# Swapping two products at the start of a seven-product up projection, and issuing one gate convolution after a bank copy

## The chip, the core and the metric

The kernel is one program on one core of a Trainium2 chip. The core has a matrix engine (TensorE, PE in the profile; its weight loads have a row of their own, PEld), a vector engine (VectorE, DVE), an activation engine (ScalarE, ACT), a general engine (GpSimd, POOL) and a queue engine (SyncE, SP). POOL and SP also issue transfers between the chip's memory and the core. Each engine works through its own list of instructions in order, and semaphores hold an instruction back until what it needs is there. The matrix engine accumulates into eight banks, each 128 by 512 float32.

The metric is the device time of one execution in microseconds (us), the median of several runs.

## The reference, cut to what matters

One layer of a streaming encoder on 512 tokens and 2048 channels, float32. The change lies in the second half, the gated feed-forward block with a causal convolution over three tokens:

```python
h  = rms_norm(x, pre_ffn_g)
up = causal_dwconv(h @ w_up, conv_w, conv_b)          # 2 x 5632 columns
y  = (gelu(up[..., :F]) * up[..., F:]) @ w_down       # F = 5632
x  = x + rms_norm(y, post_ffn_g)
```

The convolution is per column: out[t] = b + w2 z[t] + w1 z[t-1] + w0 z[t-2].

## The kernel before

**Units and blocks.** The 5632 columns are worked in 22 units of 256. A unit u has two column blocks of `w_up`: a gate block, which gets convolution and gelu (`gate`), and a linear block, which gets the convolution and is multiplied with the gate's result (`product`, which then writes the result to memory with two POOL transfers, L977, `gd<-ca`). The first three of the 44 blocks (unit 0's two and unit 1's gate) are computed by the plain routine `up`. The other 41 are numbered k = 0 to 40 and computed by seven products each. Block 0 is unit 1's linear block, block 1 is unit 2's gate block, and so on; blocks k and k + 1 overlap in the order of the work, and blocks 0 and 1 are the first pair.

**Splitting.** To reach float32 precision each operand is split into a rounded high part and a low part (`split`, L135 on ACT for the high part, L136 on DVE for the low part). Of the seven-product stage each factor of `w_up` is split into `wfh` and `wfl`, 128 by 1024 each. These live in eight buffers, four factors at a time, and four factors are prepared ahead of the product in use: the split of a factor overwrites the buffers of the factor four before it in the order, and waits until PE has read those.

**Seven products.** With h and the weight block each cut into 2 by 2 quarters, a scheme of the Strassen kind needs seven products P1 to P7 in place of eight. Each product is 8 wide matmuls with `wfh` (L159, 128x512) and 8 narrow ones with `wfl` (L165, 128x256). In `TURNED` products (P6, P7, P4) the narrow ones come first. P1, P6, P7 and P4 of one block accumulate one after the other in the same bank, named `qa`; P5 and P3 use `qg`, P2 uses `qd`. After P1, P6 and P7 the running sum in `qa` is copied out by ACT (L1159 into `za`, L1169 into `zm`, L1173 into the second half of `zm`), because a later output needs the sum up to that point. The next product on the same bank may not start until the copy has read it. So P7 waits for the copy of P6 (L1169), and P4 for the copy of P7 (L1173).

**The order of products** is the list built in `Factors.__init__`. Each product gets a key, 7k plus a place (P1 0, P2 2, P5 4, P3 6, P6 8, P7 10, P4 12), and the list is sorted by it, except for a hand-written beginning and end. Sorted, P2 of block k + 1 (key 7k + 9) falls between P6 (7k + 8) and P7 (7k + 10) of block k. The hand-written beginning of the kernel before is (block, product) (0,1), (0,2), (0,5), (1,1), (0,3), (1,2), and then the sorted rest follows: (0,6), (0,7), (1,5), (0,4), (1,3), (2,1).

PE's order is the order of the program text. The order on ACT and DVE is set by a scheduler when the program is built; `tc.issue_after(ins)` puts the instructions traced inside it behind `ins` on `ins`'s engine.

**Weights on their way.** A factor is often the sum of weight quarters. The first quarter is loaded by SP (L1089); others are added in memory order by POOL transfers that accumulate into the same tile (L1106), each issued once the split that used the previous sum is done. Of block 0, P5, P6 and P4 share the tile `wx`: the accumulating transfer for P6 follows the low-part split of P5's factor, the one for P4 follows that of P6's. P7's factor shares the tile `wy` with P3's.

**Unit 1's gate.** `gates[1] = gate(1, normed(z))` scales the plain result into `z` (L987, DVE), and `gate` runs two ACT convolution passes (L950 into `ca`), two DVE passes for each half (L951, L952) and a gelu (L964). There is one `ca` buffer, and the gate of unit 1 can only write it when the transfers that store unit 0's result (`gd<-ca`) have read it.

Of the kernel before, what the change touches and what calls it, by code (L numbers as in the profile page):

```python
# [11 lines left out]
AF = mybir.ActivationFunctionType  # L12
# [63 lines left out]
def encoder_layer(ctx: ExitStack, tc: tile.TileContext, x, xT, vecs, rel, post_mix, post_ffn,  # L76
# [7 lines left out]
    nc = tc.nc  # L84
# [48 lines left out]
    def split(hi, lo, src, scale=None):  # L133
        if scale is None:
            rounded = nc.scalar.activation(hi, src, AF.Copy)  # L135
            rest = nc.vector.tensor_sub(lo, src, f32(hi))  # L136
        else:
            rounded = nc.scalar.activation(hi, src, AF.Copy, scale=scale)
            rest = nc.vector.scalar_tensor_tensor(lo, src, scale, f32(hi), op0=ALU.mult, op1=ALU.subtract)
        split.last, split.rest = rounded.ins, rest.ins  # L140
        return rounded.ins
# [81 lines left out]
    def qk_specs(h):  # L223
        return halves(f"q{h}", w_in, head_cols("q", h), 8, P), halves(f"k{h}", w_in, head_cols("k", h), 8, P)
# [45 lines left out]
    for h in range(1, HEADS):  # L270
        q, k = qk_specs(h)
# [63 lines left out]
    for kb in range(KD):  # L335
        i, o = divmod(kb, 8)
# [22 lines left out]
    with tc.tile_pool(name="p1", bufs=2, reuse_waits="tile") as p1:  # L359
# [31 lines left out]
        def keep(what, h, ps):  # L391

            f = t512("tmp")
            nc.vector.tensor_mul(f, ps, R)
            hi, lo = t512(what + "h", F32R), t512(what + "l", F32R)
            split(hi, lo, f)
            state[what, h] = hi, lo
# [12 lines left out]
        def head(what, h):  # L410
            keep(what, h, project(f"{what}{h}"))
# [422 lines left out]
    def raw1(name, dt=F32):  # L834
        return right_tile("raw1", name, dt)
# [107 lines left out]
    def flat(v):  # L943
        return v.rearrange("p a b -> p (a b)")

    with tc.tile_pool(name="p3", bufs=2, reuse_waits="tile") as p3:
        def taps(z, b, c):

            v = [col(V_CONV, 4 * b + i) for i in range(4)]
            nc.scalar.activation(c, z, AF.Identity, scale=v[2], bias=v[3])  # L950
            nc.vector.scalar_tensor_tensor(c[:, 1:], z[:, :S - 1], v[1], c[:, 1:], op0=ALU.mult, op1=ALU.add)  # L951
            nc.vector.scalar_tensor_tensor(c[:, 2:], z[:, :S - 2], v[0], c[:, 2:], op0=ALU.mult, op1=ALU.add)  # L952

        def new_z():
            return p3.tile([P, 2, S], F32, tag="z", bufs=1, name="z")

        def gate(u, z):
            if u == NU - 1:
                a = raw1("ca")[:, :2, :]
            else:  # L960
                a = p3.tile([P, 2, S], F32, tag="ca", bufs=1, name="ca")
            for j in range(2):
                taps(z[:, j, :], 2 * u + j, a[:, j, :])
            nc.scalar.activation(flat(a), flat(a), AF.Gelu_apprx_tanh)  # L964
            return a
# [18 lines left out]
        def normed(ps):  # L984
            z = new_z()
            for j in range(2):
                nc.vector.tensor_mul(z[:, j, :], ps[j], R)  # L987
            return z

        def up(u, p, between=()):  # L990
            ps = [bank(f"up{u}_{p}_{j}") for j in range(2)]
            between = list(between)
            for i in range(4):
                w = weights.get(f"w{p}{u}_{i}")
                factors.prefetch(4 - len(weights.specs) + weights.used)
                for kb in range(4 * i, 4 * i + 4):
                    for j in range(2):
                        mm3(ps[j], part(w, j, slice(kb % 4 * P, (kb % 4 + 1) * P)), g_both(hT, kb),
                            kb == 0, kb == KD - 1)
                step = between.pop(0) if between else None  # L1000
                if step:
                    step()
            return ps
# [19 lines left out]
        def quarter(k, t, i):  # L1023

            return tuple(hT[2 * k + i][:, :, at, :] for at in AT[t])
# [7 lines left out]
        def raw_x(name):  # L1033
            return p3.tile([P, 1024], F32, tag="x", bufs=4, name=name)
# [26 lines left out]
        def h_difference():  # L1061

            for i, v in enumerate(differences):
                split(*quarter(0, 1, i), v)

        class Factors:
# [3 lines left out]
            def __init__(self):  # L1070
                n = 2 * NU - PLAIN

                self.alone = 0, n - 1
                place_of = {1: 0, 6: 8, 2: 2, 7: 10, 5: 4, 4: 12, 3: 6}
                begin = [(0, 1), (0, 2), (0, 5), (1, 1), (0, 3), (1, 2)]
                end = [(n - 1, 5), (n - 2, 6), (n - 1, 3), (n - 1, 1), (n - 2, 7), (n - 1, 6), (n - 2, 4),
                       (n - 1, 7), (n - 1, 2), (n - 1, 4)]
                order = sorted((7 * k + at, k, i) for k in range(n) for i, at in place_of.items())  # L1080
                self.order = begin + [(k, i) for _, k, i in order if (k, i) not in begin + end] + end
                self.raw, self.made, self.loaded, self.used = {}, [], 0, 0
# [59 lines left out]
        banks, gates = {}, {}  # L1142
# [6 lines left out]
        def pair_tile(tag, n, bufs=1):  # L1149
            return p3.tile([P, n, 2, T], F32, tag=tag, bufs=bufs, name=tag)  # L1150

        def wide(v):
            return v.rearrange("p a b c -> p (a b c)")

        def keep(k, i):

            if i == 1:
                zs[k, "1"] = pair_tile("za", 1, 2)
                nc.scalar.activation(wide(zs[k, "1"]), banks[k, "a"], AF.Copy)  # L1159
            elif i == 2:  # L1160
                v = wide(zs[k, "1"])
                nc.vector.tensor_add(v, banks.pop((k, "d")), v)
            elif i == 5:
                zs[k, "5"] = raw_x("zb")[:, :S] if k == end else wide(pair_tile("zb", 1))
                nc.scalar.activation(zs[k, "5"], banks[k, "g"], AF.Copy)  # L1165
            elif i == 6:
                zs[k, "m"] = pair_tile("zm", 2)
                v = wide(zs[k, "m"][:, :1])
                nc.scalar.activation(v, banks[k, "a"], AF.Copy)  # L1169
                nc.vector.tensor_add(v, banks.pop((k, "g")), v)  # L1170
            elif i == 7:
                v = wide(zs[k, "m"][:, 1:])
                nc.scalar.activation(v, banks[k, "a"], AF.Copy)  # L1173
                nc.vector.tensor_add(v, zs.pop((k, "5")), v)
            elif i == 4:
                keep_all(k)

        def keep_all(k):
            one, m, a = zs.pop((k, "1")), zs.pop((k, "m")), banks.pop((k, "a"))
            z = new_z()  # L1180
            nc.vector.tensor_add(z[:, 0, :T], one[:, 0, 0], one[:, 0, 1])
            nc.vector.tensor_add(z[:, 1].rearrange("p (a b) -> p a b", a=2), m[:, :, 0], m[:, :, 1])
            nc.scalar.activation(z[:, 0, T:], a[:, T:], AF.Copy)
            nc.vector.tensor_add(z[:, 0, T:], a[:, :T], z[:, 0, T:])
            nc.vector.tensor_mul(flat(z), flat(z), flat(RR))
            u, p = divmod(PLAIN + k, 2)
            if p:
                product(u, gates.pop(u), z)
            else:
                gates[u] = gate(u, z)  # L1190

        def seven(k, i):
            w = factors.get()
            if i in FIRST:
                banks[k, BANK[i]] = bank(f"q{BANK[i]}_{k}")
            ps = banks[k, BANK[i]]
            mm2(ps, w, [h_factor(i, kb) for kb in range(8)], i in FIRST, i in TURNED)
# [9 lines left out]
        for i in range(2):  # L1207
            h_sums(i)
        z = up(1, 0, [spread2, lambda: product(0, gate(0, normed(ups[0])), normed(ups[1]))])
        gates[1] = gate(1, normed(z))  # L1210
        rights, firsts = [right(0, cc) for cc in range(2)], []
        for r in rights:
            next(r)
# [2 lines left out]
        def next_first():  # L1216

            cc, i = ORDER0[len(firsts)]
            r = rights[cc].send(i)
            firsts.append((firsts[0][0] if firsts else first_left(), r))  # L1220

        for k, i in factors.order:
            seven(k, i)
            keep(k, i)
            if (k, i) == factors.order[0]:
                with ExitStack() as behind:
                    for ins in factors.third:
                        behind.enter_context(tc.issue_after(ins))
                    h_difference()
            if (k, i) == (end, 6):  # L1230
                summed.close()
                pr = ctx.enter_context(tc.tile_pool(name="pr", bufs=2, side="right", reuse_waits="tile"))
            if (k, i) == (end, 6):
                next_first()
            elif (k, i) == (end - 1, 4):
                next_first()
# [4 lines left out]
    with tc.tile_pool(name="p4", bufs=2, reuse_waits="tile") as p4:  # L1241
# [180 lines left out]
        for n in ("11", "12", "21", "22"):  # L1422
            for t in range(2):
# [3 lines left out]
                if n in not_stored:  # L1427
                    v = at[:, l * C + S:(l + 1) * C]
# [56 lines left out]
```

## Time and profile before

| | us |
|---|---|
| median of 3 runs | 1875.63 |
| lowest and highest run | 1873.43, 1879.35 |
| the profiled execution | 1878.7 |
| its span, first to last instruction | 1876.9 |
| PE busy in the span | 1860.8 |
| mean granted PE clock (1 is full) | 0.997 |

In rows of the timeline the first number is the start in us from the beginning of the span, the second the duration of the group, and what stands in square brackets is the idle time before it on that engine and what released it. `PEclk` is the share of full speed that PE's clock was granted. The seven-product stage begins at 636 us of the span and ends at 1443 us.

### The profile page before, as it was taken

The page shows a single profiled execution, that of the slowest core. Times are in us where ns is not written, and L with a number is a line of the kernel's source. Part 1 is how long each engine was busy: PE and PEld are TensorE (multiplying, and loading weights), DVE is VectorE, ACT ScalarE, POOL GpSimd, SP SyncE. Part 2 cuts the span into 40 slices and gives each one's busy share as a digit, 9 for nine tenths or more (in the row PEclk, how much of TensorE's full clock was granted, in tenths as well). Part 3 has the DMA queues.
Part 4 walks back from the last instruction along what each step waited for, and adds up shares of the span by engine and source line. Part 5 has one row for each costly group of instructions (what it writes and reads, how often), then busy time and mean ns, then how long its engine had stood idle before and what let it go on. Part 6 is the DMA issues. An engine that isn't in the chain of part 4 may idle for free.

```text
span 1876.9 us, 24890 instructions
## 1 busy us (share of the span) xinstructions
PE 1860.8 (99%) x9486; PEld 1592.3 (85%) x9486; DVE 1439.5 (77%) x1631; ACT 1018.8 (54%) x1287; POOL 297.9 (16%) x400
## 2 busy tenths in 40 slices
PE   9999999999999999999999999999999999999998
PEld 7888888888889888888888888888888888888886
DVE  6555445577598888888888888888887899899876
ACT  7333333246465555666656666565655665565553
POOL 5201011100000112121221212222121011111101
PEclk9999999999999999999999999999999999999999
DMA  8799599997794779889898898988989977877785
GB/s 306 238 248 239 161 261 247 246 251 259 227 303 169 182 178 202 202 206 206 201 199 200 207 208 199 198 200 208 211 171 290 349 224 177 204 202 179 174 236 151
DMA packets 181751, 409.20 MB, mean 218 GB/s; under 512 B 11456, under 2 KB 62528, under 8 KB 176320
## 3 DMA queue, kind: packets, MB, share of 16 engines
q0 software_dynamic: 52112, 156.78, 43.8%
q1 hardware_dynamic: 129520, 250.84, 39.8%
q8 instruction: 74, 1.21, 0.3%
q14 instruction: 45, 0.37, 0.1%
HBM read 361.44 MB, written 96.47 MB: 244 GB/s over the span
## 4 chain that ended last, share of the span: by engine, by line
PE 64%; issue 2%; DMA 1%; ACT 0%; DVE 0%; POOL 0%; POOLq 0%; DVEq 0%; ACTq 0%
PE qa L159 16%; PE qa L165 8%; PE qg L159 8%; PE qg L165 4%; PE pa L154 4%; PE pa L153 4%; PE pa L151 4%; PE qd L159 4%; PE pg L154 2%; PE pg L153 2%; PE pg L151 2%; PE qd L165 2%; PE pd L154 1%; PE pd L153 1%; PE pd L151 1%
## 5 line engine op out<-in xcount | busy, mean ns | idle before, releaser
L159 PE MATMUL qa<-gT,wfh 128*128 128x512 f32 x984 | 248.0, 394 | 0.0
L135 ACT ACTIVATE wfh<-wx 128x1024 fp32r<-128x1024 f32 x164 | 173.7, 1059 | 131.2 <-PE qg L159 49.7
L136 DVE TENSOR_TENSOR wfl<-wx,wfh 128x1024 fp32r<-128x1024 f32 x164 | 200.6, 1223 | 53.7 <-ACT wfh L135 36.3
L159 PEld LDWEIGHTS qa<-gT,wfh 128*128 128x128 f32 x984 | 178.1, 190 | 32.0
L1106 POOL DMA_DIRECT2D wx<-in_w_up x122 | 104.5, 857 | 511.0 <-DVE wfl L136 473.9
L159 PE MATMUL qg<-h,wfh 128*128 128x512 f32 x656 | 162.3, 389 | 0.0
L159 PEld LDWEIGHTS qg<-h,wfh 128*128 128x128 f32 x656 | 123.1, 188 | 25.7 <-ACT zb L1165 0.2
L165 PE MATMUL qa<-gT,wfl 128*128 128x256 f32 x984 | 138.9, 284 | 4.7 <-ACT zm L1169 4.7
L136 DVE TENSOR_TENSOR bl<-b,bh 128x2048 fp32r<-128x2048 f32 x56 | 127.2, 2287 | 18.7 <-ACT bh L135 11.7
L135 ACT ACTIVATE bh<-b 128x2048 fp32r<-128x2048 f32 x56 | 106.1, 1913 | 60.2 <-DVE b L870 24.3
L165 PEld LDWEIGHTS qa<-gT,wfl 128*128 128x128 f32 x984 | 130.1, 192 | 8.9 <-ACT zm L1169 5.5
L135 ACT ACTIVATE wfh<-wy 128x1024 fp32r<-128x1024 f32 x82 | 86.9, 1060 | 92.8 <-PE qg L159 50.0
L151 PE MATMUL pa<-bh,ah 128*128 128x512 f32 x320 | 124.5, 389 | 0.0
L153 PE MATMUL pa<-bl,ah 128*128 128x512 f32 x320 | 124.5, 389 | 0.0
L154 PE MATMUL pa<-bh,al 128*128 128x512 f32 x320 | 124.5, 389 | 0.0
L136 DVE TENSOR_TENSOR wfl<-wy,wfh 128x1024 fp32r<-128x1024 f32 x82 | 100.1, 1221 | 9.7 <-ACT wfh L135 5.6
L165 PEld LDWEIGHTS qg<-h,wfl 128*128 128x128 f32 x656 | 89.5, 190 | 6.4
L136 DVE TENSOR_TENSOR wfl<-wz,wfh 128x1024 fp32r<-128x1024 f32 x41 | 50.3, 1226 | 55.7 <-PE qa L159 55.7
L165 PE MATMUL qg<-h,wfl 128*128 128x256 f32 x656 | 91.5, 282 | 0.0
L159 PE MATMUL qa<-h,wfh 128*128 128x512 f32 x328 | 82.1, 392 | 0.0
L159 PE MATMUL qd<-gT,wfh 128*128 128x512 f32 x328 | 81.1, 389 | 0.0
L938 POOL DMA_DIRECT2D sum<-part x30 | 36.2, 1207 | 262.9 <-DVE part L924 191.7
(543 smaller groups left out, 4552.8 us busy)
## 6 DMA issues: line engine op xcount, KB each, us to landing
wx<-in_w_up POOLq DMA_DIRECT2D x122, 512.0 KB, 6.3
b<-in_w_down SPq DMA_DIRECT2D x32, 1024.0 KB, 7.1
wx<-in_w_up SPq DMA_DIRECT2D x43, 512.0 KB, 5.5
wz<-in_w_up SPq DMA_DIRECT2D x41, 512.0 KB, 6.1
wy<-in_w_up SPq DMA_DIRECT2D x41, 512.0 KB, 4.6
wy<-in_w_up POOLq DMA_DIRECT2D x41, 512.0 KB, 7.0
sum<-part POOLq DMA_DIRECT2D x38, 512.0 KB, 7.8
wt<-in_w_o POOLq DMA_DIRECT2D x16, 1024.0 KB, 12.8
```

What stands on the lines that cost most here:

```text
L135: rounded = nc.scalar.activation(hi, src, AF.Copy)
L136: rest = nc.vector.tensor_sub(lo, src, f32(hi))
L151: nc.tensor.matmul(ps, l[0], r[0], start=first, stop=False, skip_group_check=onto)
L153: nc.tensor.matmul(low, l[0], r[1], start=False, stop=False, skip_group_check=onto)
L154: nc.tensor.matmul(ps, l[1], r[0], start=False, stop=last, skip_group_check=onto)
L159: nc.tensor.matmul(ps, w[0][:, kb], pairs[kb][0], start=fresh and not kb, stop=last, skip_group_check=not fresh)
L165: nc.tensor.matmul(ps[:, sl], w[1][:, kb], pair[:, sl], start=False, stop=last, skip_group_check=not fresh)
L938: nc.gpsimd.dma_start(dest, v, accum_op=ALU.add)
L1106: nc.gpsimd.dma_start(self.raw[k, what], self.block(k, m, kh), accum_op=ALU.add)
```

## The change

Two edits. The hand-written beginning loses (1,2), so that the sorted rest sets its place: the order becomes (0,1), (0,2), (0,5), (1,1), (0,3), (0,6), (1,2), (0,7), (1,5), (0,4), with P2 of block 1 between P6 and P7 of block 0. And the gate of unit 1 is no longer traced ahead of the seven-product loop: its scaled input is made there as before, but the gate itself is traced after P6 of block 0 and ordered on ACT behind the copy of P6's bank (L1169). Nothing is computed in another way, and no instruction is added or removed.

```diff
-                begin = [(0, 1), (0, 2), (0, 5), (1, 1), (0, 3), (1, 2)]
+                begin = [(0, 1), (0, 2), (0, 5), (1, 1), (0, 3)]
...
                 v = wide(zs[k, "m"][:, :1])
-                nc.scalar.activation(v, banks[k, "a"], AF.Copy)
+                keep.six = nc.scalar.activation(v, banks[k, "a"], AF.Copy).ins
                 nc.vector.tensor_add(v, banks.pop((k, "g")), v)
...
         z = up(1, 0, [spread2, lambda: product(0, gate(0, normed(ups[0])), normed(ups[1]))])
-        gates[1] = gate(1, normed(z))
+        z = normed(z)
...
         for k, i in factors.order:
             seven(k, i)
             keep(k, i)
...
+            if (k, i) == (0, 6):
+                with tc.issue_after(keep.six):
+                    gates[1] = gate(1, z)
```

On PE, from P3 of block 0 to the start of its P7. In the kernel before, `qg_5453` is block 0's P3, `qd_5522` block 1's P2, and `qa_5401` block 0's bank, first P6 (with `h_5184`), then P7 (with `gT_4460`):

```order
L159 MATMUL qg_5453<-h_5183,wfh 128x512 x8
L165 MATMUL qg_5453<-h_5183,wfl 128x256 x8
L159 MATMUL qd_5522<-gT_4462,wfh 128x512 x4
L159 MATMUL qd_5522<-gT_4463,wfh 128x512 x4
L165 MATMUL qd_5522<-gT_4462,wfl 128x256 x4
L165 MATMUL qd_5522<-gT_4463,wfl 128x256 x4
L165 MATMUL qa_5401<-h_5184,wfl 128x256 x8
L159 MATMUL qa_5401<-h_5184,wfh 128x512 x8
L165 MATMUL qa_5401<-gT_4460,wfl 128x256 x4
```

The same place in the changed kernel, where the bank of block 0 is `qa_5393`, P3's is `qg_5445` and block 1's P2 has `qd_5546`:

```order
L159 MATMUL qg_5445<-h_5183,wfh 128x512 x8
L165 MATMUL qg_5445<-h_5183,wfl 128x256 x8
L165 MATMUL qa_5393<-h_5184,wfl 128x256 x8
L159 MATMUL qa_5393<-h_5184,wfh 128x512 x8
L159 MATMUL qd_5546<-gT_4462,wfh 128x512 x4
L159 MATMUL qd_5546<-gT_4463,wfh 128x512 x4
L165 MATMUL qd_5546<-gT_4462,wfl 128x256 x4
L165 MATMUL qd_5546<-gT_4463,wfl 128x256 x4
L165 MATMUL qa_5393<-gT_4460,wfl 128x256 x4
```

P6 has moved up by one product, and P2 of block 1 now stands between P6 and P7.

On ACT, from the split of P7's factor (the first `wy`) to the copy of P7, in the kernel before; the `wx` rows are the splits of block 1's P5, block 0's P4 and block 2's P1, in this order, and the second `wy` is that of block 1's P3:

```order
L135 ACTIVATE wfh<-wy 128x1024
L1159 ACTIVATE za<-qa_5478 128x512
L135 ACTIVATE wfh<-wx 128x1024
L950 ACTIVATE ca<-z,vec 128x512 x2
L135 ACTIVATE wfh<-wx 128x1024
L135 ACTIVATE wfh<-wy 128x1024
L1169 ACTIVATE zm<-qa_5401 128x512
L964 ACTIVATE ca<-ca 128x1024
L135 ACTIVATE wfh<-wx 128x1024
L1173 ACTIVATE zm<-qa_5401 128x512
```

And in the changed kernel:

```order
L135 ACTIVATE wfh<-wy 128x1024
L1159 ACTIVATE za<-qa_5470 128x512
L135 ACTIVATE wfh<-wx 128x1024 x2
L1169 ACTIVATE zm<-qa_5393 128x512
L950 ACTIVATE ca<-z,vec 128x512 x2
L135 ACTIVATE wfh<-wy 128x1024
L135 ACTIVATE wfh<-wx 128x1024
L964 ACTIVATE ca<-ca 128x1024
L1173 ACTIVATE zm<-qa_5393 128x512
```

The convolution passes of unit 1's gate (`ca<-z,vec`) and the split of block 1's P3 factor have moved from ahead of the copy of P6 (L1169) to behind it; the split of P4's factor (the second `wx`) still stands ahead of it; the gelu (L964) has moved behind the split of block 2's P1 factor, next to the copy of P7 (L1173).

On DVE, the low-part splits and the last part of unit 0's product, in the kernel before; `wz` is the factor of block 1's P2, `wx` that of block 0's P6:

```order
L974 TENSOR_TENSOR ca<-ca,cb 128x512
L136 TENSOR_TENSOR wfl<-wz,wfh 128x1024
L951 SCALAR_TENSOR_TENSOR cb<-z,vec,cb 128x511
L1162 TENSOR_TENSOR za<-qd_5430,za 128x512
L952 SCALAR_TENSOR_TENSOR cb<-z,vec,cb 128x510
L136 TENSOR_TENSOR wfl<-wx,wfh 128x1024
L974 TENSOR_TENSOR ca<-ca,cb 128x512
```

And in the changed kernel:

```order
L974 TENSOR_TENSOR ca<-ca,cb 128x512
L136 TENSOR_TENSOR wfl<-wx,wfh 128x1024
L951 SCALAR_TENSOR_TENSOR cb<-z,vec,cb 128x511
L1162 TENSOR_TENSOR za<-qd_5423,za 128x512
L952 SCALAR_TENSOR_TENSOR cb<-z,vec,cb 128x510
L136 TENSOR_TENSOR wfl<-wz,wfh 128x1024
L974 TENSOR_TENSOR ca<-ca,cb 128x512
```

The two splits have changed places. The order of the transfers on SP and on POOL is the same in both kernels.

## The prediction

> **What bounds the kernel now.** I read the page first, then the waits of PE, then PE's and ACT's timelines around the one long wait, and last the clock and the transfers there. The page's span and PE's busy time:
>
> ```profile
> span 1876.9 us, 24890 instructions
> PE 1860.8 (99%) x9486; PEld 1592.3 (85%) x9486; DVE 1439.5 (77%) x1631; ACT 1018.8 (54%) x1287; POOL 297.9 (16%) x400
> ```
>
> PE is idle for only 16.1 us of the span, so a change pays only where it moves PE's idle time or PE's rate. The waits of PE name one such place in the seven-product stage:
>
> ```profile
> PE qa L165 <- ACT zm L1169: 4.7, 2, 3.7
> ```
>
> Two waits for the copy of P6 (L1169), 3.7 us and 1.0 us. PE's timeline shows where the long one is (P2 of block 1, then P6 narrow, P6 wide, P7 narrow, P7 wide, P5 of block 1 wide and narrow, P4 narrow):
>
> ```profile
> 649.91 2.00 PE L159 MATMUL qd<-gT,wfh 128*128 128x512 f32 x8
> ...
> 652.70 1.12 PE L165 MATMUL qa<-h,wfl 128*128 128x256 f32 x8
> 653.66 2.00 PE L159 MATMUL qa<-h,wfh 128*128 128x512 f32 x8
> 659.35 2.07 PE L165 MATMUL qa<-gT,wfl 128*128 128x256 f32 x8 [3.69 <-ACT zm L1169]
> 661.22 3.62 PE L159 MATMUL qa<-gT,wfh 128*128 128x512 f32 x8
> 664.64 2.13 PE L159 MATMUL qg<-h,wfh 128*128 128x512 f32 x8
> 666.61 1.11 PE L165 MATMUL qg<-h,wfl 128*128 128x256 f32 x8
> 667.56 1.12 PE L165 MATMUL qa<-gT,wfl 128*128 128x256 f32 x8
> ```
>
> It is P7 of block 0. Besides the idle time, the matmuls after it are long: eight narrow ones take 661.22 - 659.35 = 1.87 us where P6's took 0.96, eight wide ones 3.42 us. The second pair, which already has P2 between P6 and P7, gives the measure:
>
> ```profile
> 676.87 2.00 PE L159 MATMUL qa<-h,wfh 128*128 128x512 f32 x8
> 678.71 1.98 PE L159 MATMUL qd<-gT,wfh 128*128 128x512 f32 x8
> ...
> 681.48 1.12 PE L165 MATMUL qa<-gT,wfl 128*128 128x256 f32 x8
> ```
>
> Eight wide ones take 1.84 us, a product 2.8, and P7 starts without a wait. The clock explains the rest; the windows' last three columns are granted clock, DMA share and GB/s:
>
> ```profile
> 640.00:655.00 15.00, 15.00 (x90) 13.33 (x89) 10.41 (x13) 5.92 (x7) 4.87 (x6) 1.00 1.00 263
> ...
> 658.50:664.50 6.00, 5.15 (x16) 4.47 (x17) 4.29 (x6) 2.80 (x4) 0.87 (x1) 0.50 0.47 115
> ```
>
> After the wait PE ran at half its clock. So the wait has two prices. Idle: P6's wide matmuls are through at 653.66 + 1.84 = 655.50, P7 starts at 659.35: 3.85 us. Half rate: 1.87 - 0.96 = 0.91, 3.42 - 1.84 = 1.58 and, for P5, 1.97 - 1.84 = 0.13: 2.6 us. Together 6.5 us, 0.35% of the span.
>
> Why the copy is late is in ACT's timeline:
>
> ```profile
> 640.77 1.07 ACT L135 ACTIVATE wfh<-wz 128x1024 fp32r<-128x1024 f32 x1 [1.24 <-PE qd L159]
> ...
> 643.57 1.06 ACT L135 ACTIVATE wfh<-wx 128x1024 fp32r<-128x1024 f32 x1 [0.69 <-PE qg L159]
> ...
> 649.80 1.06 ACT L135 ACTIVATE wfh<-wy 128x1024 fp32r<-128x1024 f32 x1 [4.68 <-DMA wy<-in_w_up]
> ...
> 651.24 1.05 ACT L135 ACTIVATE wfh<-wx 128x1024 fp32r<-128x1024 f32 x1
> 655.41 1.52 ACT L950 ACTIVATE ca<-z,vec 128x512 f32<-128x512 f32 x2 [3.12 <-DMA gd<-ca]
> 656.83 1.04 ACT L135 ACTIVATE wfh<-wx 128x1024 fp32r<-128x1024 f32 x1
> 657.78 1.04 ACT L135 ACTIVATE wfh<-wy 128x1024 fp32r<-128x1024 f32 x1
> 658.73 0.57 ACT L1169 ACTIVATE zm<-qa 128x512 f32<-128x512 f32 x1
> 660.82 1.06 ACT L964 ACTIVATE ca<-ca 128x1024 f32<-128x1024 f32 x1 [1.52 <-DVE ca L952]
> 661.78 1.04 ACT L135 ACTIVATE wfh<-wx 128x1024 fp32r<-128x1024 f32 x1
> 664.88 0.60 ACT L1173 ACTIVATE zm<-qa 128x512 f32<-128x512 f32 x1 [2.06 <-PE qa L159]
> ```
>
> The bank was full at 655.5, but ACT stood until 655.41 before the gate's convolution, which waits for the store of unit 0's result, and then worked through convolution and two splits.
>
> **The change part by part.** *PE's order.* P6 takes P2's start, 649.91; P2 of block 1 follows at 652.70, P7 is due at 655.50, block 1's P5 at 658.3, P4 at 661.1 (it started at 667.56, 6.5 us later).
>
> *P6's factor, split one place earlier.* Its last quarter is an accumulating transfer on POOL:
>
> ```profile
> 634.61 0.88 POOL L1106 DMA_DIRECT2D wx<-in_w_up  x1 [23.31 <-DVE wfl L136]
> ...
> 641.66 0.86 POOL L1106 DMA_DIRECT2D wy<-in_w_up  x1 [0.93 <-DVE wfl L136]
> 646.45 0.86 POOL L1106 DMA_DIRECT2D wx<-in_w_up  x1 [3.93 <-DVE wfl L136]
> 647.06 1.74 POOL L977 DMA_DIRECT2D gd<-ca  x2
> ```
>
> The landing of the first, asked for alone, of the two stores, and of all 163 accumulating ones:
>
> ```profile
> DMA to landing us min/median/max: 6.7/6.7/6.7
> ```
>
> ```profile
> DMA to landing us min/median/max: 7.5/7.5/7.6
> ```
>
> ```profile
> DMA to landing us min/median/max: 5.3/6.6/9.6
> ```
>
> It is there at 634.61 + 6.7 = 641.3; the split ends at 642.4, its low part on DVE at about 643.7, and P6 needs both at 649.91. Cost nothing, with 6 us of cover. The transfer behind it, for P4's factor, is then issued at about 643.9 instead of 646.45. The POOL queue keeps its order (behind `wy` of 641.66, ahead of the stores), so nothing is pushed behind more bytes. SP's next load into the tile that P2's factor frees goes out about one product, 2.8 us, later; its reader stands eleven products behind, 30 us, and its queue keeps its order. Cost nothing.
>
> *The copy of P6.* Ahead of it on ACT now stand only splits: P7's (649.80, held by the transfer of 641.66, which the change leaves alone), block 1's P5 (651.24) and P4's. P4's split needs its transfer, which by the range of landings is there between 643.9 + 5.3 = 649.2 and 653.5, and P6's buffers, which PE gives up at 652.70. I take 652.9, at latest 653.6; one split (656.83 to 657.78) is 0.95, so the copy runs from 653.85 to 654.4, at latest to 655.15. P7 is due at 655.50: the wait goes, cover 0.35 to 1.1 us. With it goes its half-rate stretch, since no idle time is left ahead of it.
>
> *The gate, behind the copy.* It waits for the stores, in before until 655.41. Unit 0's last multiplication on DVE now stands behind the low part of P6's factor instead of P2's; the high part before it ends at 642.4 instead of 641.84 (640.77 + 1.07), so the stores go out up to 0.6 us later, unless the earlier transfer ahead of them helps. The gate's convolution starts between 654.4 (right behind the copy) and 656.0; I take the old 655.4. Then come 1.4 us for it, 0.95 for block 1's P3 split, and from 658.3 + 0.2 the split of block 2's P1 factor, which waits for P7's wide matmuls: until 659.45. Gelu 0.95, copy of P7 0.6: about 661.0 against P4's start at 661.1. Gelu's DVE input is no later, since two foreign instructions leave that chain:
>
> ```profile
> 646.07 0.69 DVE L974 TENSOR_TENSOR ca<-ca,cb 128x512 f32<-128x512 f32 x1
> ...
> 656.92 0.68 DVE L1162 TENSOR_TENSOR za<-qd,za 128x512 f32<-128x512 f32 x1
> ...
> 658.84 1.22 DVE L136 TENSOR_TENSOR wfl<-wx,wfh 128x1024 fp32r<-128x1024 f32 x1
> 659.98 0.74 DVE L952 SCALAR_TENSOR_TENSOR ca<-z,vec,ca 128x510 f32<-128x510 f32 x1
> ```
>
> Without them the last pass ends near 659.0 instead of 660.7. P4 may still wait between 0 and 1.9 us (gelu at its old 660.82 puts the end of P7's copy at 662.4, 1.3 late, and 0.6 for late stores). I take 0.1, nearest to the chain as added up. Who needs the gate itself is the product with block 0's result, which only follows P4's end at 663.9.
>
> *Sum.* -3.85 - 2.6 + 0.1 = -6.35 us, between -6.45 and -4.55. From 664 us on the order is the old one, and the stage ran there on PE alone but for the 1.0 us wait, so all of it arrives at the end: span 1870.5, and 1.8 us around it, 1872.3 against the profiled 1878.7. That execution lies 3.1 us above the median of the three runs and within their limits; off the median, 1875.63 - 6.35 gives 1869.3 us.
>
> [...] The rows show one wait of 3.7 us followed by 0.50 of the clock, and no second case. [...]
>
> **The rivals.** *The half-rate stretch is not in the runs that set the median.* Then only the idle 3.85 us are to be had there, less the 0.1: 1871.9. For it: a wait this short was followed by half rate in one profiled execution, and the three runs spread over 5.9 us. Against it: that execution is itself an ordinary one. [...]
>
> *The wait moves to P4.* The gate now stands between the copies of P6 and P7. If the stores land 2 us late, the chain above gives P4 a wait of some 2.5 us: 1875.63 - 6.45 + 2.5 = 1871.7. For it: transfers run at a DMA share of 1.00 from 640 to 655, and my chain has 0.1 us to spare. Against it: their bytes and order are the same.
>
> *Slower.* The split of P4's factor, which waits for a transfer, stands ahead of the copy of P6, so a late transfer holds P7. To lose 5.6 us on before, P7 must start at 655.50 + 3.85 + 5.6 = 665 (half rate as before), so the transfer must land at 663.4, 19.5 us after its issue. The longest of 163 took 9.6. It would give 1881.2 or more.
>
> **How the numbers follow.** Forecast 0.58 (1869.3, own range 1866.5 to 1872), no half rate to save 0.20, wait at P4 0.15, slower 0.07, which holds the spread of runs too. 0.3% is 5.6 us, about what a measurement of this kernel can tell from no change; the forecast clears it by 0.7 us, with runs 3 us to either side. Of the forecast's 0.58 I give 0.45 to faster and 0.13 to within; of the two partial cases together 0.10 to faster. Faster 0.55, same 0.38, slower 0.07. The range, 1865.8 to 1876.0, reaches from the whole 6.5 us with the runs 3.3 lower to no gain.
>
> **What would show it.** In the profile after: no wait of P7 at 655.5 us and no line "qa L165 <- ACT zm L1169" of 3.7 us; a clock of 1.00 from 655 to 665; P4 at 661 to 662; the copy of P6 done by 655.2; the gate's convolution at 654.4 to 656. A wait of P4 for L1173 over 1 us would show the second rival, a copy of P6 after 656 the third, and a before whose runs keep full clock after the wait the first. The forecast is wrong if the stage's end, 1443 us, comes less than 4 us earlier.

## The result

The changed kernel took 1872.2 us (median of 22 runs, 1869.37 to 1875.16); the kernel before, run beside it, 1877.13 us (22 runs, 1873.24 to 1879.37). The ratio is 0.9977, with a 95% interval of 0.9970 to 0.9983: a gain of 0.23%, or 4.3 us (3.2 to 5.6); the two medians are 4.9 us apart, the two means 4.4. So it is faster, as the interval does not reach 1, and the upper end of the gain touches the 5.6 us (0.3%) that the prediction took as about what a measurement can tell from no change. The time lies in the range given and 2.9 us above the forecast.

The page of the profiled execution of the changed kernel, and the waits of PE that are left in it:

```profile
span 1867.6 us, 24890 instructions
PE 1857.1 (99%) x9486; PEld 1590.2 (85%) x9486; DVE 1437.1 (77%) x1631; ACT 1020.2 (55%) x1287; POOL 297.8 (16%) x400
```

```profile
PE idle L128 <- DVE early L120: 1.1, 1, 1.1
PE q L151 <- ACT q_0h L135: 0.3, 1, 0.3
PE q L153 <- DVE hT L139: 0.3, 1, 0.3
```

The line of L165 waiting for L1169, 4.7 us in the kernel before, in two waits, is gone. This execution took 1869.37 us, the shortest of the 22, so the 9.3 us between it and the profiled execution of before are not the gain. PE's timeline at the place (P6 narrow and wide, P2 of block 1, P7, P5 of block 1, P4 of block 0):

```profile
648.74 1.12 PE L165 MATMUL qa<-h,wfl 128*128 128x256 f32 x8
649.70 2.00 PE L159 MATMUL qa<-h,wfh 128*128 128x512 f32 x8
651.54 1.98 PE L159 MATMUL qd<-gT,wfh 128*128 128x512 f32 x8
653.35 1.12 PE L165 MATMUL qd<-gT,wfl 128*128 128x256 f32 x8
654.30 1.12 PE L165 MATMUL qa<-gT,wfl 128*128 128x256 f32 x8
655.26 2.00 PE L159 MATMUL qa<-gT,wfh 128*128 128x512 f32 x8
657.10 1.98 PE L159 MATMUL qg<-h,wfh 128*128 128x512 f32 x8
658.92 1.11 PE L165 MATMUL qg<-h,wfl 128*128 128x256 f32 x8
659.87 1.12 PE L165 MATMUL qa<-gT,wfl 128*128 128x256 f32 x8
```

No row has a wait, the wide matmuls of P7 take 1.84 us again, and P4 starts 659.87 - 634.80 = 25.07 us after the stage's first product (P1 of block 0, at 634.80 here, 635.97 in before); in before it was 667.56 - 635.97 = 31.59 us. ACT's timeline over the same stretch:

```profile
648.96 1.05 ACT L135 ACTIVATE wfh<-wx 128x1024 fp32r<-128x1024 f32 x1
652.39 1.06 ACT L135 ACTIVATE wfh<-wx 128x1024 fp32r<-128x1024 f32 x1 [2.39 <-DMA wx<-in_w_up]
653.35 0.58 ACT L1169 ACTIVATE zm<-qa 128x512 f32<-128x512 f32 x1
653.83 1.51 ACT L950 ACTIVATE ca<-z,vec 128x512 f32<-128x512 f32 x2
655.25 1.05 ACT L135 ACTIVATE wfh<-wy 128x1024 fp32r<-128x1024 f32 x1
656.20 1.04 ACT L135 ACTIVATE wfh<-wx 128x1024 fp32r<-128x1024 f32 x1
658.04 1.06 ACT L964 ACTIVATE ca<-ca 128x1024 f32<-128x1024 f32 x1 [0.81 <-DVE ca L952]
659.01 0.58 ACT L1173 ACTIVATE zm<-qa 128x512 f32<-128x512 f32 x1
```

The copy of P6 is through at 653.93, 0.37 us ahead of P7; the gate's convolution follows right behind it; the copy of P7 is through at 659.59, 0.28 us ahead of P4. The granted clock (third number from the right) stays whole through the stretch:

```profile
655.00:658.00 3.00, 3.00 (x16) 2.52 (x15) 3.00 (x6) 2.24 (x3) 0.00 (x0) 1.00 0.92 253
658.00:661.00 3.00, 3.00 (x22) 2.83 (x21) 3.00 (x4) 2.49 (x3) 0.87 (x1) 1.00 0.16 37
```

So the mechanism came out as forecast, 6.5 us at the place between these two executions, and yet the runs differ by 4.3 us. The experiments ask where the other 2 us are.

### The profile page after: what moved, and what is told of

Read it like the earlier page. It is cut to its first block, busy times and chain, and to the rows that moved or that the text cites. A ratio compares the mean times of both kernels' runs of the same rounds, so it can differ in the third digit from the quotient of the medians.

```text
span 1867.6 us, 24890 instructions
## 1 busy us (share of the span) xinstructions
PE 1857.1 (99%) x9486; PEld 1590.2 (85%) x9486; DVE 1437.1 (77%) x1631; ACT 1020.2 (55%) x1287; POOL 297.8 (16%) x400
## 4 chain that ended last, share of the span: by engine, by line
PE 98%; DVE 1%; ACT 1%; DMA 0%; SPq 0%; issue 0%; POOL 0%; DVEq 0%; POOLq 0%; ACTq 0%
PE qa L159 16%; PE qa L165 8%; PE qg L159 8%; PE qg L165 4%; PE qd L159 4%; PE pa L153 4%; PE pa L154 4%; PE pa L151 4%; PE m L154 3%; PE m L151 3%; PE m L153 3%; PE qd L165 2%; PE pg L153 2%; PE pg L154 2%; PE pg L151 2%; PE u L151 2%
## 5 line engine op out<-in xcount | busy, mean ns | idle before, releaser
L165 PE MATMUL qa<-gT,wfl 128*128 128x256 f32 x984 | 137.7, 283 | 0.0
L165 PEld LDWEIGHTS qa<-gT,wfl 128*128 128x128 f32 x984 | 129.4, 191 | 3.4
L151 PE MATMUL pa<-bh,ah 128*128 128x512 f32 x320 | 124.5, 389 | 0.0
L165 PEld LDWEIGHTS qg<-h,wfl 128*128 128x128 f32 x656 | 89.5, 190 | 6.4
L165 PE MATMUL qg<-h,wfl 128*128 128x256 f32 x656 | 91.5, 282 | 0.0
```

The costliest lines, as they stand in the source:

```text
L151: nc.tensor.matmul(ps, l[0], r[0], start=first, stop=False, skip_group_check=onto)
L165: nc.tensor.matmul(ps[:, sl], w[1][:, kb], pair[:, sl], start=False, stop=last, skip_group_check=not fresh)
```

## The experiments

Theory A: the place costs the kernel before a different amount in each run, because its wait and the half-rate stretch vary; the change takes all of it. Theory B: the place always cost 6.5 us, and the change gives some of it back elsewhere. Theory C, for the changed kernel alone: P4 takes over some of the wait.

In what follows a profile is one profiled execution (a "look" in the expectations); "first profile" means the one of before or of the changed kernel that stands above. To compare them, each is cut at three rows of PE's timeline: the start of the stage, the start of P4 of block 0 (the place), and the first matmul of the down projection (L151, the stage's end). In the first profile of the changed kernel P7 starts 19.50 us after the stage's start and P4 25.07 us after it. "Idle" is by how much P7 starts later than those 19.50 us, "half rate" what the place costs beyond 25.07 us and the idle part. Where the clock stayed whole behind a wait, 0.08 to 0.09 us stand in this column too, since the first narrow matmuls after a wait take some 1.05 us instead of 0.96.

| execution | stage starts at | place | idle | half rate | rest of stage | from stage's end to end of span |
|---|---|---|---|---|---|---|
| before | 635.97 | 31.59 | 3.88 | 2.64 | 775.94 | 433.40 |
| same_a | 636.44 | 30.22 | 3.48 | 1.67 | 775.07 | 433.37 |
| same_b | 636.63 | 30.35 | 3.78 | 1.50 | 775.28 | 433.44 |
| same_c | 636.44 | 31.35 | 3.40 | 2.88 | 776.08 | 433.43 |
| same_d | 635.28 | 30.16 | 3.41 | 1.68 | 774.47 | 433.39 |
| same_e | 635.64 | 31.05 | 4.32 | 1.66 | 775.35 | 433.46 |
| same_f | 636.57 | 30.35 | 3.87 | 1.41 | 774.48 | 433.40 |
| fill | 637.01 | 28.64 | 3.49 | 0.08 | 774.39 | 433.36 |
| order_only | 636.50 | 27.34 | 2.18 | 0.09 | 774.41 | 433.45 |
| gate_only | 635.75 | 26.04 | 0.88 | 0.09 | 776.89 | 433.42 |
| changed | 634.80 | 25.07 | 0 | 0 | 774.30 | 433.43 |
| after_b | 638.29 | 25.08 | 0.01 | 0 | 775.71 | 433.42 |
| after_c | 636.58 | 25.07 | 0.01 | 0 | 775.90 | 433.45 |
| after_d | 635.62 | 25.07 | 0 | 0 | 775.70 | 433.41 |

**The kernel before, again (same_a).** No edit.

> The kernel before, unchanged, for a second look at its wait of P7. Theory A (the half-rate stretch depends on the moment at which the wait falls): the wait of P7 for the copy of P6 is again 3 to 4 us, but the granted clock after it may be 0.50 for some 6 us or 1.00; where it is 1.00 the place costs 3.9 us, not 6.5. Theory B (the gain of the change was real in full, 6.5 us, and about 2 us were given back behind the stage): clock 0.50 again, 6.5 us lost at the place in this look too. Time the same as before, ratio 1.000.

1876.88 us, ratio 1.0003 (0.9994 to 1.0012). The place cost 30.22 us, 1.4 us less than in the first profile of before. Half of theory A's idea shows in PE's timeline:

```profile
654.13 2.00 PE L159 MATMUL qa<-h,wfh 128*128 128x512 f32 x8
659.42 1.21 PE L165 MATMUL qa<-gT,wfl 128*128 128x256 f32 x8 [3.29 <-ACT zm L1169]
660.47 3.56 PE L159 MATMUL qa<-gT,wfh 128*128 128x512 f32 x8
663.83 2.05 PE L159 MATMUL qg<-h,wfh 128*128 128x512 f32 x8
```

The wait is nearly the same, but the eight narrow matmuls right after it still take 1.05 us; only then does the clock fall, and the wide ones take 3.36. So the half rate did not come and go, as theory A had it; it came at another moment, and cost 1.7 us in place of 2.6.

**The idle time filled (fill).** The wait stays, but PE works through most of it on zeros, into a bank of its own; the 14 matmuls are 28 records in the trace.

```diff
         for k, i in factors.order:
+            if (k, i) == (0, 7):
+                spare = bank("spare")
+                for _ in range(14):
+                    nc.tensor.matmul(spare[:, :P], early, early, start=True, stop=True)
             seven(k, i)
```

> The kernel before with 14 matmuls of 128x128 on zeros into a spare bank between P6 and P7 of block 0, so that PE works through most of its 3.85 us wait: the wait stays, the idle time goes. Theory A: no half-rate stretch; P7 starts at the same time as before; gain against a look with half rate 2.6 us, against the mean of before's runs less than that, 0.5 to 1.5 us (ratio 0.9992 to 0.9997). Theory B: gain 2.6 us (ratio 0.9986).

```profile
654.71 2.01 PE L159 MATMUL qa<-h,wfh 128*128 128x512 f32 x8
656.56 3.29 PE L1226 MATMUL spare<-early 128*128 128x128 f32 x28
660.00 1.21 PE L165 MATMUL qa<-gT,wfl 128*128 128x256 f32 x8 [0.15 <-ACT zm L1169]
661.04 2.00 PE L159 MATMUL qa<-gT,wfh 128*128 128x512 f32 x8
```

```profile
658.00:661.00 3.00, 2.85 (x25) 2.65 (x24) 3.00 (x5) 1.95 (x3) 0.00 (x0) 1.00 0.78 134
```

P7 starts as late as before (3.49 us late), and everything after it runs at full rate; the granted clock is 1.00 where the kernel before had 0.51. The ratio is 0.9996 (0.9987 to 1.0005), 11 runs against 33. That lies in theory A's range, and theory B's 0.9986 lies just outside the interval; but the interval holds no change as well as the 1.9 us that the half rate cost in the mean of the seven profiles of before. That the stretch of half rate comes from the idle time is shown by this trace, one against seven; its price is not settled by this run's time.

**The order alone (order_only).**

```diff
-                begin = [(0, 1), (0, 2), (0, 5), (1, 1), (0, 3), (1, 2)]
+                begin = [(0, 1), (0, 2), (0, 5), (1, 1), (0, 3)]
```

> Only the list is changed (P2 of block 1 between P6 and P7); the gate stays ahead of the copy of P6 on ACT. Both theories: P6 ends 2.8 us earlier and the stores land earlier, but the copy still stands behind the gate's convolution and one split; P7 waits 0.5 to 1.5 us at a clock of 1.00, so the place costs that instead of 6.5 us. Theory A: ratio 0.998 to 0.9985; theory B: 0.997 to 0.998.

```profile
655.18 1.52 ACT L950 ACTIVATE ca<-z,vec 128x512 f32<-128x512 f32 x2 [3.07 <-DMA gd<-ca]
656.61 1.04 ACT L135 ACTIVATE wfh<-wx 128x1024 fp32r<-128x1024 f32 x1
657.55 0.57 ACT L1169 ACTIVATE zm<-qa 128x512 f32<-128x512 f32 x1
```

P7 waited 2.0 us, more than the 0.5 to 1.5 expected, since the stores of unit 0's result, and the gate behind them, were hardly earlier here: the gate began 18.7 us after the stage's start, 19.4 in the first profile of before. There is no half rate in this profile, and its place is 3.4 us cheaper than the mean of before. The ratio is 0.9993 (0.9984 to 1.0002), a smaller gain than either theory had, 1.3 us (none to 3.0). In 4 of the 11 timed runs the mean granted clock was 0.997 and in those the mean time 1875.9 us, against 1874.2 us in the others. This may be half rate after a wait of some 2 us in some runs, but no trace shows it, and the mean clock is a loose sign: one run of after_b below has 0.953 at an ordinary 1873.44 us.

**The gate alone (gate_only).** `begin` as before, the rest of the change as it is.

> Only the gate is moved behind the copy of P6; P7 follows P6 directly as before. The copy can only begin when P6 ends, and the split of block 1's P3 factor, which waits for P6's buffers, stands ahead of it: P7 waits 1.0 to 2.0 us, at a clock of 1.00. Theory A: ratio 0.998 to 0.9990; theory B: 0.997 to 0.998.

```profile
654.47 1.04 ACT L135 ACTIVATE wfh<-wy 128x1024 fp32r<-128x1024 f32 x1
655.49 0.60 ACT L1169 ACTIVATE zm<-qa 128x512 f32<-128x512 f32 x1
655.98 1.51 ACT L950 ACTIVATE ca<-z,vec 128x512 f32<-128x512 f32 x2
```

The copy follows P6's end by 0.2 us, and P7 waits 0.69 us, less than expected: the split of block 1's P3 factor runs from 654.47, while P6's wide matmuls are still at work, so it does not wait for those. P6's narrow ones were through by then, at 653.45. The ratio, 0.9979 (0.9970 to 0.9988), cannot be told from that of the whole change, and it lies at the border of the two theories' ranges. The move of the gate carries most of the gain, 4.7 of the 5.65 us at the place; with the gate moved, the order adds the other 0.97 us, which no time here resolves.

**The changed kernel, again (after_b, after_c, after_d).** No edit.

> The changed kernel, unchanged, looked at again. The place (from P1 to P4 of block 0) takes 25.1 us where no wait is left, 31.6 and 30.2 us in the two looks at before; the rest of the stage took 774.3 to 775.9 us, the tail 433.4 us in every look, and the stage began at 634.8 to 637.0 us. Theory A (before's cost at the place varies with its wait and clock, the change always takes all of it): 25.1 us at the place, 774.3 for the rest; a time above that of the first look (1869.4 us) comes from a stage that begins later than 634.8 us. Theory B (part of the gain is given back): the place is 25.1 us in each look, but the rest of the stage is 775.5 to 777 us in some, by a wait of PE for ACT behind the place. Theory C: P4 waits for the copy of P7 in some looks and the place is 25.5 to 27 us.

> As for after_b: A: place 25.1, rest 774.3; B: place 25.1, rest 775.5 to 777; C: place 25.5 to 27 us.

> As for after_b: A: place 25.1, rest 774.3; B: place 25.1, rest 775.5 to 777; C: place 25.5 to 27 us.

The place is 25.07 or 25.08 us in each, and P4 never waits: theory C falls. The rest of the stage is 775.7 to 775.9 us, 1.4 to 1.6 us above the first profile, with short waits of PE behind the place, here those of after_d and after_b from 664 to 1450 us:

```profile
PE qg L159 <- ACT zb L1165: 0.9, 1, 0.9
```

```profile
PE qa L165 <- ACT zm L1169: 0.8, 2, 0.5
```

That is what theory B expected, but the kernel before has such waits too, none to 1.0 us in a profile, and the profiles of before below have the same rest. after_b was also timed: 1872.18 us, ratio 0.9977 (0.9967 to 0.9987), the same as the first time.

**Five more profiles of before (same_b to same_f).**

> The kernel before once more. If its cost at the place varies between looks (theory A): anything from 28.5 us (a wait of some 3.4 us at full clock) to 31.6 us. If it is always the whole of idle time and half rate (theory B): 30 to 31.6 us, with a clock of 0.50 for 3 to 6 us.

> The kernel before again, for what the place costs it from run to run. Three looks gave 31.6, 30.2 and 30.4 us from P1 to P4, so 5.1 to 6.5 us over the 25.1 us of the changed kernel, while the timed runs of the two kernels differ by 4.3 us (3.2 to 5.6). Theory A (the place is dearer in some runs than in others, the rest does not care): looks with 28 to 30 us must turn up, and the rest of the stage stays at 774 to 776 us. Theory B (the change gives back 1 to 2 us elsewhere): the place costs 30 to 31.6 us again, and the rest of before is 1 us shorter than that of the changed kernel (775.4 us in the mean of four looks).

> As for same_c: A: 28 to 31.6 us at the place, rest 774 to 776; B: 30 to 31.6 us, rest near 774.4.

> As for same_c: A: 28 to 31.6 us at the place, rest 774 to 776; B: 30 to 31.6 us, rest near 774.4.

> As for same_c: A: 28 to 31.6 us at the place, rest 774 to 776; B: 30 to 31.6 us, rest near 774.4.

The place cost 30.16 to 31.35 us, never less than 30. Two of them, same_c with the half rate at the wait's own end, and same_f with its end within P7's wide matmuls:

```profile
659.34 2.08 PE L165 MATMUL qa<-gT,wfl 128*128 128x256 f32 x8 [3.20 <-ACT zm L1169]
661.22 3.62 PE L159 MATMUL qa<-gT,wfh 128*128 128x512 f32 x8
664.63 2.38 PE L159 MATMUL qg<-h,wfh 128*128 128x512 f32 x8
```

```profile
659.94 2.08 PE L165 MATMUL qa<-gT,wfl 128*128 128x256 f32 x8 [3.67 <-ACT zm L1169]
661.82 2.48 PE L159 MATMUL qa<-gT,wfh 128*128 128x512 f32 x8
664.13 2.00 PE L159 MATMUL qg<-h,wfh 128*128 128x512 f32 x8
```

The granted clock of same_c and then of same_f (third number from the right) shows where the factor of two comes from:

```profile
658.00:661.00 3.00, 1.66 (x7) 1.66 (x8) 3.00 (x5) 1.48 (x3) 0.00 (x0) 0.60 0.41 81
661.00:664.00 3.00, 3.00 (x9) 2.42 (x9) 1.78 (x3) 1.80 (x2) 0.87 (x1) 0.50 0.75 195
664.00:667.00 3.00, 3.00 (x12) 2.37 (x12) 2.04 (x3) 0.60 (x1) 0.56 (x1) 0.76 0.87 160
```

```profile
658.00:661.00 3.00, 1.06 (x5) 1.06 (x6) 3.00 (x5) 1.89 (x3) 0.00 (x0) 0.73 0.52 100
661.00:664.00 3.00, 3.00 (x13) 2.58 (x13) 2.37 (x4) 2.01 (x2) 0.87 (x1) 0.70 0.52 183
664.00:667.00 3.00, 3.00 (x19) 2.62 (x18) 2.52 (x3) 1.44 (x2) 0.85 (x1) 1.00 0.96 146
```

Taking the clock as either 1.00 or 0.50 at each moment (in before it is 0.50 over the whole of 658.5 to 664.5 us), the time at half rate is 6 us times what a window lacks to 1.00, summed: (0.40 + 0.50 + 0.24) x 6 = 6.84 us in same_c, (0.27 + 0.30) x 6 = 3.42 us in same_f. The same sum gives 6.84 us for before and 3.42 us for each of the other four: in these seven profiles a stretch came in one length or in twice that length. What it cost is close to half of the part of it in which PE had work. In same_f it began at 661 - 0.27 x 6 = 659.38, 0.56 us ahead of P7, so 2.86 us were left and cost 1.43 (1.41 in the table); in same_c it began at 658.60, 0.74 us ahead of P7, and 6.10 us were left, half of which is 3.05 (2.88 in the table).

Over the seven profiles the idle part is 3.73 us in the mean and the half-rate part 1.92 (1.41 to 2.88): the place costs 30.72 us, 5.65 over the changed kernel. The profiles are from more than one chip, but same_b and after_b to after_d share one, and there the place is 30.35 against 25.07 to 25.08 us. The rest of the stage is 775.24 us in the mean of before and 775.40 of the changed kernel, the start 636.14 and 636.32 us: no give-back that could be told from their scatter, which is 1.6 us from the lowest rest to the highest in either kernel. Place, rest and start together make the profiles differ by 5.3 us, which lies in the interval of the timed runs, 3.2 to 5.6. Theory B falls in its main point, that the place always costs 6.5 us; a give-back of up to some 1 us is not ruled out. Theory A holds for the size of the half-rate part, not for its absence. Between 5.3 and the 4.3 us of the timed runs stays 1 us that these profiles do not settle.

## Why the prediction was right or wrong, point by point

- **The bound, the place and the cause.** Right. The copy of P6 stood behind the gate's convolution on ACT, the gate behind the stores; with the gate behind the copy and a product between, the wait goes, in four profiles of four. P4 was due 661.1 - 635.97 = 25.1 us after the stage's start, and came at 25.07.
- **The half-rate term.** The step that failed is the term of the sum "Half rate: ... 2.6 us", which was taken from one execution. It was one of the two largest of seven, the two in which the stretch had its double length; the mean of the seven is 1.92 us. The idle term, 3.85 us, was 3.73 in the mean. So the sum of 6.35 us was 0.7 us too large at the place.
- **From the sum to the time.** The forecast took 6.35 us off a median of three runs, 1875.63 us; 22 runs gave 1877.13. These 1.5 us are half of the 2.9 us by which the forecast lies too low; the other 1.4 are the 6.35 us of the sum against the 4.9 between the medians. With the gain at 4.3 us, 0.23%, the result is on the near side of 0.3%, which had a chance of 0.38; "faster by over 0.3%", with 0.55, did not come.
- **The cover of the copy of P6.** Right in its outcome, wrong in one of its reasons. P4's split on ACT did not wait for all of P6: in after_d it began at 651.26, while P6's wide matmuls ran from 650.52 to 652.36. Nor does such a split wait, as the section on the kernel before has it, until PE has read both buffers of the factor four before it. Here and in gate_only the split on ACT began after P6's narrow matmuls and ahead of the end of its wide ones, which fits one of the two buffers being free by then; no run tests it. P4's split was held by its transfer, which landed 9.7, 9.7, 9.8 and 7.3 us after its issue in the four profiles, in three of them past the 9.6 that I had taken as the upper end. The cover at P7 was 0.37, 0.25, 0.58 and 1.96 us, against the 0.35 to 1.1 I had worked out.
- **The gate behind the copy.** Right. It started right behind the copy in three profiles and waited 1.23 us for the stores in one; these landed 6.0 to 7.3 us after their issue instead of 7.5 to 7.6. P4's 0.1 us was nil in each, with 0.2 to 1.0 us to spare.
- **The rivals.** "The half-rate stretch is not in the runs that set the median" was wrong as put, as far as profiles can tell: it is in all seven; only its price differs, 1.41 to 2.88 us for waits of 3.2 to 4.1 us. In the seven profiles the stretch began at no fixed distance from the wait: from 1.3 us before P7's start (before) to 1.1 us after it (same_a, same_d), and from 2.4 us (before, where PE was idle from 655.66 and the clock fell at 661 - 0.49 x 6 = 658.06) to 4.4 us (same_a, same_e) after PE's idle time had begun. It lasted 3.42 us or twice that. What sets the moment and the length is not shown. The wait at P4 and the slower case did not come, although the transfer that the slower case rests on came later, in three profiles of four, than any of the 163 of before. The 2.5 us that the second rival gives for stores 2 us late do not come out of the chain as added up from 655.4, which gives 1.9.

## What to carry to other kernels

On an engine that serves a matmul chain in order, put first what the chain waits for: here a 0.6 us copy stood behind a convolution that nobody needed until after P4. When the clock falls behind a stall, read the price from several executions, since the idle part stayed between 3.4 and 4.3 us while the half-rate part changed by a factor of two. And take the base from as many runs as the gain is small: three runs of this kernel were 1.5 us off, a third of what the change brought.

## What the runs showed that was not expected

The stretch of half rate came in two lengths only, 3.42 and 6.84 us; the long one came in the two profiles where the clock fell 0.74 us or more ahead of P7 (before, same_c), the short one where it fell at most 0.56 us ahead of it or later. The clock also fell after the work had begun again: in same_a the eight narrow matmuls behind a 3.29 us wait took 1.05 us, and the half rate began with the wide ones. A wait of 3.2 us (same_c, same_d) was as good for a half-rate stretch as one of 4.13 us (same_e), and the shortest of these waits paid the most, 2.88 us. Whether a wait of 2 us can draw one is not shown: the one trace of such a wait, order_only's, has none.
